# One store moved from ScalarE's DMA queue to SyncE's, behind the last load, in a split-GELU kernel

## The chip, the cores and the metric

The kernel runs on one core of a Trainium2 chip. The metric is the time on the device in microseconds (us), the median of several runs.

The core has five instruction engines. Three matter here: ScalarE (ACT in the profile) computes GELU, VectorE (DVE) multiplies, SyncE (SP) only issues DMAs. A DMA issued by SyncE stands in the profile's queue q1, one issued by ScalarE in q10. All queues are served by the core's 16 DMA engines. A DMA engine moves its part of a DMA in packets, and ends it with a packet of 4 bytes, called its closing write here: the 35 DMAs of the kernel before leave 560 of them, 16 each. In the traces a DMA lands with its last closing write (the store of tile 14 in the kernel before: closing write at 459.3 us, landing at 459.4).

## The reference

```python
x: (32, 512, 2048) float32
x1, x2 = x[..., :1024], x[..., 1024:]
out = 0.5 * x1 * (1 + erf(x1 / sqrt(2))) * x2     # (32, 512, 1024) float32
```

The input is 134 MB and the output 67 MB. There are only two elementwise steps between them.

## The kernel before

The input is cut into 16 tiles. A tile has 128 partitions with 8 rows of 2048 numbers each: 8 MB in, 4 MB out. Two buffers hold input tiles and two hold output tiles. SyncE issues the loads, two tiles ahead. ScalarE issues the stores, except those of the last tile, which go to SyncE in four pieces of 1 MB as the pieces become ready.

```python
xpool = ctx.enter_context(tc.tile_pool(name="xpool", bufs=2))
opool = ctx.enter_context(tc.tile_pool(name="opool", bufs=2))

def load(i):
    x_tile = xpool.tile([P, R, dim], x.dtype, name="x_tile")
    nc.sync.dma_start(out=x_tile, in_=x_t[i])
    return x_tile

ahead = [load(0), load(1)]
for i in range(n_tiles):                       # 16 tiles, R = 8
    x_tile = ahead.pop(0)
    o_tile = opool.tile([P, R, half], out.dtype, name="o_tile")
    last = i == n_tiles - 1
    pieces = 4 if last else 1
    step = R // pieces
    for k in range(pieces):
        for r in range(k * step, (k + 1) * step):
            nc.scalar.activation(              # GELU in place
                out=x_tile[:, r, :half], in_=x_tile[:, r, :half], func=GELU
            )
            nc.vector.tensor_mul(
                out=o_tile[:, r, :],
                in0=x_tile[:, r, :half], in1=x_tile[:, r, half:],
            )
        rows = slice(k * step, (k + 1) * step)
        queue = nc.sync if last else nc.scalar
        queue.dma_start(out=o_t[i][:, rows, :], in_=o_tile[:, rows, :])
    if i + 2 < n_tiles:
        ahead.append(load(i + 2))
```

Of the kernel before, what the change touches and what calls it, by code (L numbers as in the profile page):

```python
# [1 line left out]

# [4 lines left out]

GELU = mybir.ActivationFunctionType.Gelu


@with_exitstack
def kernel(
    ctx: ExitStack,
    tc: tile.TileContext,
    x: bass.AP,
    out: bass.AP,
):




    nc = tc.nc
    P = nc.NUM_PARTITIONS

    x_flat = x.flatten_outer_dims()
    out_flat = out.flatten_outer_dims()
    n_rows, dim = x_flat.shape
    half = dim // 2

    R = 8  # L30
    x_t = x_flat.rearrange("(n p r) d -> n p r d", p=P, r=R)
    o_t = out_flat.rearrange("(n p r) d -> n p r d", p=P, r=R)
    n_tiles = x_t.shape[0]
# [10 lines that stand above are left out]
    for i in range(n_tiles):  # L44
# [7 lines that stand above are left out]
                nc.scalar.activation(  # L52
# [4 lines that stand above are left out]
                    in0=x_tile[:, r, :half],  # L57
                    in1=x_tile[:, r, half:],
                )
            rows = slice(k * step, (k + 1) * step)  # L60
            queue = nc.sync if last else nc.scalar
            queue.dma_start(out=o_t[i][:, rows, :], in_=o_tile[:, rows, :])
        if i + 2 < n_tiles:
            ahead.append(load(i + 2))


# [1 line left out]
_INS = ['x']  # L68
_OUTS = [((32, 512, 1024), 'float32')]


# [23 lines left out]
```

## Time and profile before

The time was 472.1 us (472.06 to 473.35 in 3 runs). This is what matters, and where it is read:

| what | value | view |
|---|---|---|
| span of the profiled run | 470.3 us | page |
| VectorE / ScalarE busy | 31% / 26% | page, part 1 |
| bytes moved | 201.35 MB, mean 428 GB/s | page, part 2 |
| rate in a tile period of 29.0 us | 434 GB/s | windows |
| packet time of the two data queues, per DMA engine | 467.2 us | packet records |
| issue of load 15 to its landing | 47.65 us | chain of waits |
| closing wait of SyncE for the last store | 5.4 us | waits of SyncE |

From the page of the kernel before: the DMA row gives the mean busy share of the 16 DMA engines in tenths (9 is 90% or more) for 40 equal slices of the span. A queue line gives packets, megabytes and share of the 16 engines' time.

```profile
DVE  0070704307042070520606116060250702407034
DMA  8999999999999999999999999999999999999998
...
q1 hardware_dynamic: 2880, 138.41, 68.4%
q10 hardware_dynamic: 2160, 62.92, 31.0%
HBM read 134.22 MB, written 67.11 MB: 428 GB/s over the span
...
out_dram<-o_tile SPq DMA_DIRECT2D x4, 1024.0 KB, 5.6
```

(Names like L62 are lines of the kernel; edits make the numbers a few higher in other runs.) The two queues together take 99.4% of the DMA engines' time, and VectorE rests most of the time. The windows view of the kernel before shows a middle stretch; after the busy times of the engines come the DMA share and the rate in GB/s:

```profile
347.50:376.50 29.00, 9.17 (x8) 7.68 (x8) 0.00 (x0) 1.00 1.00 434
376.50:405.50 29.00, 9.17 (x8) 7.68 (x8) 0.00 (x0) 1.00 1.00 434
```

The DMA engines are full (1.00). The Trainium skill, "DMA: Bandwidth & Descriptors", section "Specifications", gives 435 GB/s as the ceiling of the fabric, and the measured 434 GB/s is next to it.

The chain of waits gives the last load as start, length, and what:

```profile
405.50 47.65 DMA x_tile<-in_x_dram
```

The timeline of the kernel before shows the end (start, length, engine, instruction, and in brackets how long the engine had been idle and what ended it):

```profile
434.50 0.34 ACTq L62 DMA_DIRECT2D out_dram<-o_tile  x1
453.23 7.68 ACT L52 ACTIVATE x_tile<-x_tile 128x1024 f32<-128x1024 f32 x8 [21.34 <-DMA x_tile<-in_x_dram]
454.32 9.17 DVE L55 TENSOR_TENSOR o_tile<-x_tile 128x1024 f32<-128x1024 f32 x8 [19.85 <-ACT x_tile L52]
456.70 7.14 SPq L62 DMA_DIRECT2D out_dram<-o_tile  x4
```

The first line is the store of tile 14 on ScalarE's queue. Tile 15 is computed from 453.23 to 463.5 us. The last small store is issued at 463.5 us (the fourth of the last line, which ends at 463.84). After it SyncE waits for the last landing, in its view of waits (total, times, longest):

```profile
SPq L90 <- DMA out_dram<-o_tile: 5.4, 1, 5.4
```

### The profile page before, as it was taken

The page shows a single profiled execution, that of the slowest core. Times are in us where ns is not written, and L with a number is a line of the kernel's source. Part 1 is how long each engine was busy: PE and PEld are TensorE (multiplying, and loading weights), DVE is VectorE, ACT ScalarE, POOL GpSimd, SP SyncE. Part 2 cuts the span into 40 slices and gives each one's busy share as a digit, 9 for nine tenths or more (in the row PEclk, how much of TensorE's full clock was granted, in tenths as well). Part 3 has the DMA queues.
Part 4 walks back from the last instruction along what each step waited for, and adds up shares of the span by engine and source line. Part 5 has one row for each costly group of instructions (what it writes and reads, how often), then busy time and mean ns, then how long its engine had stood idle before and what let it go on. Part 6 is the DMA issues. An engine that isn't in the chain of part 4 may idle for free.

```text
span 470.3 us, 408 instructions
## 1 busy us (share of the span) xinstructions
DVE 146.7 (31%) x128; ACT 124.2 (26%) x129; POOL 0.2 (0%) x4
## 2 busy tenths in 40 slices
DVE  0070704307042070520606116060250702407034
ACT  1050605106050150601406024060330603206042
POOL 0000000000000000000000000000000000000000
DMA  8999999999999999999999999999999999999998
GB/s 357 446 446 382 429 443 424 463 404 443 426 446 421 443 415 449 413 443 424 457 429 435 438 438 415 426 438 435 440 440 418 449 438 435 424 443 432 418 410 351
DMA packets 5042, 201.35 MB, mean 428 GB/s; under 512 B 560, under 2 KB 560, under 8 KB 560
## 3 DMA queue, kind: packets, MB, share of 16 engines
q1 hardware_dynamic: 2880, 138.41, 68.4%
q10 hardware_dynamic: 2160, 62.92, 31.0%
q14 instruction: 2, 0.02, 0.0%
HBM read 134.22 MB, written 67.11 MB: 428 GB/s over the span
## 4 chain that ended last, share of the span: by engine, by line
DMA 81%; DVE 15%; ACT 2%; DVEq 0%; issue 0%; SPq 0%; ACTq 0%
DMA x_tile<-in_x_dram 81%; DVE o_tile L55 15%; ACT x_tile L52 2%; DVEq L90 0%; SPq L40 0%; ACTq L52 0%
## 5 line engine op out<-in xcount | busy, mean ns | idle before, releaser
L55 DVE TENSOR_TENSOR o_tile<-x_tile 128x1024 f32<-128x1024 f32 x128 | 146.7, 1218 | 316.8 <-ACT x_tile L52 316.8
L52 ACT ACTIVATE x_tile<-x_tile 128x1024 f32<-128x1024 f32 x128 | 122.9, 1042 | 336.0 <-DMA x_tile<-in_x_dram 336.0
L52 ACT ACT_TABLE_LOAD x1 | 1.3, 1283 | 0.7 <-PEq L79 0.7
L79 POOL MEMSET const-bfloat16-1.0<- 128x1 bf16 x1 | 0.1, 102 | 0.0
L79 POOL MEMSET const-uint8-127<- 128x1 uint8 x1 | 0.1, 102 | 0.0
L79 POOL MEMSET const-float32-1.0<- 128x1 f32 x1 | 0.1, 99 | 0.0
L79 POOL MEMSET const-float32-0.0<- 128x1 f32 x1 | 0.1, 98 | 0.2 <-issue 0.2
## 6 DMA issues: line engine op xcount, KB each, us to landing
out_dram<-o_tile ACTq DMA_DIRECT2D x15, 4096.0 KB, 39.4
out_dram<-o_tile SPq DMA_DIRECT2D x4, 1024.0 KB, 5.6
x_tile<-in_x_dram SPq DMA_DIRECT2D x16, 47.6
```

Of the source, the lines that this page charges most:

```text
L52: nc.scalar.activation(out=x_tile[:, r, :half], in_=x_tile[:, r, :half], func=GELU)
L55: nc.vector.tensor_mul(out=o_tile[:, r, :], in0=x_tile[:, r, :half], in1=x_tile[:, r, half:],)
L79: nc = _bacc.Bacc("TRN2", target_bir_lowering=False, num_devices=1)
```

## The change

The idea is to get the store of tile 14 out of the way of the last load. On ScalarE's queue it alternates with that load, packet by packet. Behind the load in SyncE's own queue it has to wait until the load is through. The last tile should then arrive and be computed earlier.

```diff
             rows = slice(k * step, (k + 1) * step)
-            queue = nc.sync if last else nc.scalar
+            queue = nc.sync if i >= n_tiles - 2 else nc.scalar
             queue.dma_start(out=o_t[i][:, rows, :], in_=o_tile[:, rows, :])
```

## The prediction

> **What bounds the kernel now.** The 16 DMA engines. The page gives 201.35 MB at a mean of 428 GB/s over the 470.3 us span; the DMA row shows 9 in 38 of 40 slices. Summed over the packet records of the two data queues, packet time is 467.2 us per engine. The first packet starts at 2.1 us and the last ends at 469.4 us, so no engine is ever without work. VectorE is busy 31%, ScalarE 26%. The chain of waits names x_tile loads for 81%, but a load lasts 47.6 us only because it shares the engines with stores; the windows view shows 434 GB/s in each 29.0 us tile period.
>
> **How the two queues share.** The Trainium skill, "DMA: Bandwidth & Descriptors", sections "Issuing engines are not separate DMA queues" and "Queues, rings and completion order", says that all issuing engines' DMAs run on the same 16 DMA engines, each taking its queues in turn, packet by packet. This trace agrees: while both queues have work, an engine alternates a 65,536-byte load packet (2.418 us) with a 32,768-byte store packet (1.213 us).
>
> **What the change moves.** Nothing is removed or added: the 4 MB store of tile 14 goes from ScalarE's queue to SyncE's, behind load 15 and ahead of tile 15's four 1 MB stores. Its issue stays at 434.5 us, when VectorE ends tile 14: SyncE issued load 15 at 405.5 us and is free.
>
> On the DMA engines only the order changes. Store 13 empties ScalarE's queue at 441.9 to 444.8 us. Now store 14 alternates with load 15 from there; after the change load 15 has the engines to itself. On the slowest engines three store packets (3 x 1.213 = 3.6 us) leave its path. Load 15 should land at about 449.7 us, not 453.14 (44.2 us after issue, not 47.65). Tile 15's GELU and multiply move 3.4 us earlier, and VectorE ends near 460.1 us, not 463.5.
>
> **How much is critical.** None. Already now the last 1 MB store is issued at 463.5 us and waits behind others of its queue until 466.9 us, so 3.4 us of lead only lengthens that wait. After load 15, store 14 needs 8 x 1.213 = 9.7 us per engine and ends at about 459.4 us, as now; the four small stores need 4 x 2.45 us and end at 469.4 us, as now. One gap exists: eight engines end store 14 early and take about 1.2 us for their first 8 KB packet, not 0.309. It may vanish, but the engines that end last don't have it, so at most some tenths come off.
>
> **Predicted time.** 472.0 us, 8 times in 10 within 471.2 to 473.0. Chances: faster by over 2% 0.01, within 2% 0.97, slower by over 2% 0.02.
>
> **What the profile would show.** Right: load 15 lands 44 to 45 us after issue; the idle time of ScalarE before tile 15 falls from 21.3 to about 18 us; ScalarE's queue is empty from about 445 us; the four small stores take 7 to 9 us to land instead of 5.6; the store of tile 14 lands 25 us after issue, as now; total packet time and the last landing stay. Wrong: a gap in the DMA engines between load 15 and store 14, or an issue on SyncE held up.
>
> **What would make it wrong.** If switching from load to store within one queue leaves the engines idle (about 1 us); if one queue alone moves large packets slower than two together; if SyncE's queue cannot hold load 15, store 14 and the small stores, and a late issue opens a gap at the end.

## The result, and the profile after

After the change the median was 471.81 us (471.47 to 472.24, 4 runs), before 472.22 us over 4 runs, one of them run beside the kernel after. The ratio is 0.9987, 95% interval 0.9969 to 1.0005: no difference is shown. Ratios here and below are the mean time of one kernel's runs over that of the other's runs of the same rounds, so not quite the ratio of the medians quoted. Executions over 1.5% slower than the fastest of the same kernel are left out of the means.

The lines of the page that answer to those of before:

```profile
DVE  0070704307052070520705216061150702507061
DMA  8999999999999999999999999999999999999987
...
q1 hardware_dynamic: 3024, 142.61, 70.4%
q10 hardware_dynamic: 2016, 58.72, 28.9%
HBM read 134.22 MB, written 67.11 MB: 428 GB/s over the span
...
out_dram<-o_tile SPq DMA_DIRECT2D x1, 4096.0 KB, 24.7
out_dram<-o_tile SPq DMA_DIRECT2D x4, 1024.0 KB, 8.9
```

4.2 MB have moved from q10 to q1, and the sum is the same. The small stores now land 8.9 us after their issue instead of 5.6. The last load in the chain of waits, and the end in the timeline:

```profile
406.07 43.98 DMA x_tile<-in_x_dram
```

```profile
435.06 25.70 SPq L63 DMA_DIRECT2D out_dram<-o_tile  x5
450.14 7.68 ACT L53 ACTIVATE x_tile<-x_tile 128x1024 f32<-128x1024 f32 x8 [17.68 <-DMA x_tile<-in_x_dram]
451.23 9.17 DVE L56 TENSOR_TENSOR o_tile<-x_tile 128x1024 f32<-128x1024 f32 x8 [16.19 <-ACT x_tile L53]
```

The load came 3.67 us sooner (47.65 - 43.98), and VectorE ended at 460.4 us instead of 463.5. (The whole trace after is shifted by 0.57 us at the issue of load 15, 406.07 against 405.50, which is why the two differences are not the same.) The closing wait of SyncE, in its view of waits:

```profile
SPq L91 <- DMA out_dram<-o_tile: 8.7, 1, 8.7
```

So the last store is issued 3.1 us earlier (463.84 against 435.06 + 25.70 = 460.76 us, where its issue ends), and SyncE waits 3.3 us longer for it (8.7 - 5.4); the last landing is 0.2 us later in this trace.

The packet records (start, duration, size and queue of each DMA packet, put on the same time axis by the landing of load 15) say why:

| packet records | before | after |
|---|---|---|
| packet time of the two data queues, per engine | 467.2 us | 467.1 us |
| first packet starts / last packet ends | 2.1 / 469.4 us | 2.1 / 469.5 us |
| last closing write of the load 15 | 453.1 us | 450.1 us |
| last closing write of the store of tile 14 | 459.3 us | 459.7 us |
| longest 8 KB packet | 1.387 us | 0.309 us |

The DMA engines had the same packets to do and did them one after the other, in another order. The load moved forward and the store's packets back.

One small thing did change. Before, on eight engines the first 8 KB packet of tile 15's first store took 0.985 to 1.387 us instead of 0.309; after, none did. The five engines that ended last before (469.16 to 469.36 us) all had such a packet; the last engine without one ended at 469.14 us. So by this trace some tenths of a microsecond could come off. After, 15 engines had ended by 468.9 us, and one ended at 469.5 us. The times (0.6 us less, interval 1.5 less to 0.2 more) do not show whether anything came off.

### The profile page after: what moved, and what is told of

It reads as the page before. It is cut to its first block, busy times and chain, and to the rows that moved or that the text cites. A ratio compares the mean times of both kernels' runs of the same rounds, so it can differ in the third digit from the quotient of the medians.

```text
span 470.5 us, 408 instructions
## 1 busy us (share of the span) xinstructions
DVE 146.7 (31%) x128; ACT 124.2 (26%) x129; POOL 0.2 (0%) x4
## 4 chain that ended last, share of the span: by engine, by line
DMA 80%; DVE 15%; ACT 2%; DVEq 0%; issue 0%; SPq 0%; ACTq 0%
DMA x_tile<-in_x_dram 80%; DVE o_tile L56 15%; ACT x_tile L53 2%; DVEq L91 0%; SPq L41 0%; ACTq L53 0%
## 6 DMA issues: line engine op xcount, KB each, us to landing
out_dram<-o_tile SPq DMA_DIRECT2D x1, 4096.0 KB, 24.7
```

## The experiments

Two explanations stand against each other. The theory: while the DMA engines are full, the order of their packets is free, and the lead of the last tile's compute is kept as slack, time by which the last store could be issued later without harm. The rivals: the lead was worth something and was eaten, either by a single queue being slower than two or by the small stores standing behind the large one; or the last tile's compute has nothing to do with the end at all. Except where the text says otherwise each was timed in 5 rounds against the kernel before (before_mul6 and after_half14 have 4 runs).

| run | median us | ratio to before (95%) |
|---|---|---|
| before_mul3 | 474.12 | 1.0036 (1.0023 to 1.0048) |
| after_mul3 | 472.31 | 0.9998 (0.9985 to 1.0010) |
| before_mul6 | 477.83 | 1.0114 (1.0100 to 1.0128) |
| after_mul6 | 474.36 | 1.0043 (1.0030 to 1.0057) |
| before_half14 | 469.27 | 0.9937 (0.9925 to 0.9950) |
| after_half14 | 467.42 | 0.9895 (0.9881 to 0.9908) |
| pieces_pool | 472.56 | 1.0005 (0.9992 to 1.0019) |
| pieces_scalar | 472.22 | 0.9991 (0.9978 to 1.0005) |
| all_sync | 475.40 | 1.0067 (1.0054 to 1.0080) |
| sync_last4 | 472.96 | 1.0014 (1.0000 to 1.0028) |
| sync_last8 | 474.13 | 1.0033 (1.0021 to 1.0046) |
| all_sync_again | 475.84 | one look only, state unknown |

### Where the lead went: slack, measured by delaying the compute

The multiply of the last row of tile 15 is done 4 or 7 times instead of once, which delays the last store and changes no result. It was done to both kernels. The edit, shortened:

```diff
-                nc.vector.tensor_mul(...)
+                for _ in range(4 if last and r == R - 1 else 1):   # mul6: 7
+                    nc.vector.tensor_mul(...)
```

> Before, with the multiply of the last row of tile 15 done 4 times instead of once (right result): VectorE ends 3 x 1.22 = 3.66 us later, at 467.2 us. Theory: the last small store has about 0.8 us of slack before the change (it could start at 466.9 us, and an issue needs about 2.6 us to its first data), so it lands 5.3 us after its issue, at 472.5 us, and the time grows by about 3 us to 475.1 us. Rival (the compute of the last tile is no part of the end at all): no change.

> After, with the same 3 multiplies more: VectorE ends at 464.1 us. Theory: the slack is now about 4 us, so nothing is lost: 472.0 us, at most 0.3 us more. The 3.4 us that the change won are here, as slack. Rival (the gain was lost to something else, a slower queue, and isn't kept as slack): as much slower as before_mul3.

> Before, with the multiply of the last row of tile 15 done 7 times: VectorE ends 7.3 us later, at 470.8 us. Theory: the last store lands at 476.1 us, time about 478.8 us.

> After, with the same 6 multiplies more: VectorE ends at 467.7 us. Theory: the last store lands at 473.0 us, time about 475.6 us: 3.2 us less than before_mul6, the whole of what the change won for the last tile's compute.

All four were correct. The same delay cost the kernel before 1.7 us and 5.4 us, the kernel after nothing and 2.0 us (each the ratio less one, times the mean of before, 472.4 us). The direction of each was as expected; the growth expected over 472.1 us was 1.3 to 1.5 us too large in three of four. The reason is one term. An issue into an empty queue was expected to land 5.3 us later, the shortest value in the kernel before. That value still contained waiting. With the queue really empty it is 3.8 us: the timeline and the closing wait of before_mul6 show it,

```profile
454.32 16.73 DVE L56 TENSOR_TENSOR o_tile<-x_tile 128x1024 f32<-128x1024 f32 x14 [19.81 <-ACT x_tile L52]
456.70 14.70 SPq L63 DMA_DIRECT2D out_dram<-o_tile  x4
```

```profile
SPq L91 <- DMA out_dram<-o_tile: 3.4, 1, 3.4
```

and so does the listing of that line's DMAs, with the shortest, median and longest time to landing:

```profile
DMA to landing us min/median/max: 3.8/5.5/24.6
```

With the queue empty the closing wait was 3.4 us, in before_mul3, before_mul6 and after_mul6 alike. What it is longer is slack: 5.4 - 3.4 = 2.0 us before, 8.7 - 3.4 = 5.3 us after. The waits of after_mul3 and after_mul6 agree, 5.0 us with part of the slack used and 3.4 us with all of it:

```profile
SPq L92 <- DMA out_dram<-o_tile: 5.0, 1, 5.0
SPq L92 <- DMA out_dram<-o_tile: 3.4, 1, 3.4
```

The multiplies held VectorE 12.95 - 9.17 = 3.78 us (timeline of before_mul3) and 16.73 - 9.17 = 7.56 us longer:

```profile
454.39 12.95 DVE L56 TENSOR_TENSOR o_tile<-x_tile 128x1024 f32<-128x1024 f32 x11 [19.84 <-ACT x_tile L52]
```

The slack taken from these gives what should be lost:

| | delay | less slack | measured |
|---|---|---|---|
| before_mul3 | 3.78 | 1.8 | 1.7 |
| before_mul6 | 7.56 | 5.6 | 5.4 |
| after_mul3 | 3.78 | 0 | -0.1 |
| after_mul6 | 7.56 | 2.3 | 2.0 |

The rival that the last tile's compute has no part in the end falls with before_mul6, and the one that the lead was lost to something else falls with after_mul3. The change did what it was made to do, and 3.3 us of slack is what it bought.

### When the lead is worth time

Only rows 0 to 3 of tile 14 are stored, in both kernels. Their outputs are wrong, which doesn't matter for the times. It takes 2 MB of store out of the place where the lead was hidden.

```diff
             rows = slice(k * step, (k + 1) * step)
+            if i == n_tiles - 2:
+                rows = slice(0, R // 2)
```

> Before, but only rows 0 to 3 of 8 of tile 14 are stored (wrong result on purpose): 2 MB, 4 x 1.213 = 4.85 us of packet time per engine, are taken away. Theory: load 15 still alternates with the store and lands at about 453 us, VectorE ends at 463.5 us, and the last small store then finds an empty queue and lands 5.3 us later, at 468.8 us: only 0.6 us come off, 471.5 us. Rival (time follows the bytes whatever the order): 467.3 us.

> After the change, with the same 2 MB of tile 14 not stored (wrong result on purpose). Theory: load 15 lands at 450 us, VectorE ends at 460.4 us, the last small store lands about 5.3 us later, at 465.7 us: about 3.7 us come off, 468.2 us. So with the DMA engines no longer full at the end, the change is worth about 3.3 us (before_half14 against this). Rival (the earlier compute is of no worth at all, whatever else): the same time as before_half14.

The time went down by 3.0 us in the kernel before and by 5.0 us in the kernel after, so with the DMA engines no longer full at the end the change is worth 2.0 us (medians: 469.27 against 467.42, 1.85 us). That is the direction expected, but both sizes were misjudged: 0.6, 3.7 and 3.3 us were expected. The windows view of before_half14, the stretch after load 15 landed:

```profile
452.00:456.00 4.00, 2.80 (x3) 3.89 (x5) 0.00 (x0) 1.00 0.21 90
456.00:460.00 4.00, 4.00 (x4) 3.79 (x5) 0.00 (x0) 1.00 0.93 387
```

and the same of after_half14:

```profile
452.00:456.00 4.00, 4.00 (x5) 4.00 (x5) 0.00 (x0) 1.00 0.80 336
456.00:460.00 4.00, 4.00 (x4) 1.54 (x2) 0.00 (x0) 1.00 1.03 426
```

Before, the DMA engines stand at 0.21 of their time for 4 us, because there is nothing left to do until tile 15's first piece is ready. After, the store of tile 14 fills that place. The kernel after took off 5.0 us for 4.8 us of packet time per engine (8 packets of 1.213 us became 8 of 0.611 us). It was not quite full to the end, though: 15 of its engines paused between 453.3 and 454.7 us, for 0.2 to 1.3 us, until the first small store's packets came. From there the packets of the four small stores follow one another to the end, 454.6 to 464.7 us, and in before_half14 likewise from 456.8 to 467.0 us. So in both it is the first of the four small stores, not the last, whose start sets the end; it was issued at 455.59 us before and 453.33 us after, 2.3 us earlier. The kernel before took off more than expected for two reasons. The half store goes in 8 packets of 16 KB per engine, not in 4 of 32 KB, so it takes a smaller part of each turn from load 15, which now lands after 45.82 us instead of 47.65 us, in the chain of waits:

```profile
406.21 45.82 DMA x_tile<-in_x_dram
```

(3 store packets x 0.602 us shorter = 1.8 us.) And the landing after the last issue was again taken as 5.3 us; here SyncE's closing wait is 4.1 us (3.4 us with an empty queue), since the last store still stands behind the others.

### Would the small stores have to overtake the large one?

The four stores of tile 15 were given another queue than the store of tile 14. First GpSimd's:

```diff
-            queue = nc.sync if i >= n_tiles - 2 else nc.scalar
+            queue = nc.gpsimd if last else nc.sync if i == n_tiles - 2 else nc.scalar
```

> As after the change, but the four 1 MB stores of tile 15 go to GpSimd's queue, so that they need not wait behind the store of tile 14 but alternate with it. Theory: the small stores land earlier than the 8.9 us of after, but the store of tile 14 ends later by as much; 472 us within 0.3%, up to 1 us more if GpSimd's queue starts late. Rival (the 3.4 us won for tile 15's compute are lost only because its stores stand in one queue behind the store of tile 14): 469 us.

It gave 472.56 us, the same as before. But it isn't the test it was meant to be: the packet records show the first small store starting only 4.9 us after its issue, when the store of tile 14 was down to its last packets. So a second run used ScalarE's queue, which was empty by then (the edit shortened):

```diff
+            if last:   # on ScalarE's queue, piece k - 1 is issued after piece k's GELUs
+                if k > 0:
+                    nc.scalar.dma_start(<rows of piece k - 1>)
+                if k == pieces - 1:
+                    nc.scalar.dma_start(<rows of piece k>)
+                continue
             queue = nc.sync if i >= n_tiles - 2 else nc.scalar
```

> pieces_pool did not do what it was meant to: GpSimd's queue took 4.9 us to its first packet, when the store of tile 14 was nearly done. Here the small stores go to ScalarE's empty queue, each issued one piece late so that ScalarE does not stop for VectorE: the first should start near 455 us, in the middle of the store of tile 14, and alternate with it. Theory (order is free while the DMA engines are full): the first small store lands 1 us or more earlier than in after (462.1 us), the store of tile 14 ends about 1.2 us later (4 small packets of 0.309 us in between), the last small store lands at 469.4 us as ever, and the time is 472.2 us within 0.3%. Rival (the lead of tile 15's compute is lost only because its stores stand behind that of tile 14 in one queue): about 469 us.

The time was 472.22 us, as expected, but again the small stores hardly overtook. The timeline of pieces_scalar has the first of them issued at

```profile
453.87 0.34 ACTq L65 DMA_DIRECT2D out_dram<-o_tile  x1
```

and its first packet starts at 458.2 us, 4.3 us later, not near 455 us. It got between the last packets of the store of tile 14, which ended 1.0 us later than after the change (460.7 against 459.7 us), and landed no earlier for it (462.5 against 462.2 us). In before_mul6, where the engines were idle, the first packet came 1.2 us after the issue (472.3 after 471.1). The first store of the kernel before is like pieces_scalar: issued by ScalarE at 32.93 us, while a load keeps the engines busy, it has its first packet at 37.6 us, 4.7 us later. So in these traces a queue that had just been filled did not get its turn at once while another one kept the engines busy; 4 to 5 us of the other's packets went first. (The 1.2 us are of SyncE's queue; no run measured ScalarE's or GpSimd's with idle engines.) The Trainium skill, "DMA: Bandwidth & Descriptors", section "Queues, rings and completion order", has the engine take its queues in turn packet by packet. In the middle of this kernel the records agree (one 64 KB packet, one 32 KB packet, and so on); at the start of a queue they show this delay beside it.

What follows: giving the small stores their own queue brings nothing, in two runs. Whether they would bring something if they really overtook remains open. The sum of packet times says no, but no run here shows it.

### Is one queue as good as two? The miss

> Every store, not only that of tile 14, goes to SyncE's queue, so loads and stores follow one another in one queue all through: 16 changes from load to store where the change made one. Theory (the DMA engines are never without work, so the order of the same packets is free): 472.0 us, within 0.3% of before, load 15 landing near 450 us as after the change. Rival (one queue that carries both loads and stores loses time at each change of direction, and this ate the gain of the change): about 1 us or more per tile, so 485 us or more.

```diff
-            queue = nc.sync if i >= n_tiles - 2 else nc.scalar
+            queue = nc.sync
```

This expectation failed. Moving every store to SyncE's queue took 475.40 us, 3.2 us more than before by the ratio. It isn't the 13 us of the rival, but the order is not entirely free. The page of all_sync shows the DMA row full except for its last slice:

```profile
DMA  8999999999999999999989999999999999999996
```

The mean over the 16 engines hides where the loss is. The closing writes of each DMA, one per engine, show it: some engines fall behind the others. Three more runs measured how it grows:

> The stores of the last 4 tiles go to SyncE's queue (3 whole-tile stores where the change moved one), the others stay on ScalarE's. all_sync moved 15 and took 3.0 us more, with one DMA engine ending 0.9 us after all others and 3.9 us after the first. If each turn from load to store in one queue costs the same, 3 of 15 give 0.6 us more than before: 473.0 us. If the cost comes only after many turns (in all_sync the spread of the engines began to grow at about the sixth load): 472.4 us, as before.

> The stores of the last 8 tiles go to SyncE's queue: 7 whole-tile stores. If each turn costs the same: 1.4 us more than before, 473.8 us. If the cost comes only after about six turns: at most 0.5 us more.

> all_sync once more, for a second trace: if the late DMA engine is what this order makes and no accident of one execution, the spread of the 16 engines' closing writes grows again from about 0.5 us at the first loads to over 3 us at load 15, and the time is 475 to 476 us; before keeps its spread near 2 us from the second load on.

Their edits are `n_tiles - 4` and `n_tiles - 8` in place of `n_tiles - 2`, and all_sync unchanged.

| kernel | large stores on SyncE's queue | time over before | mean end of the 16 engines after the first packet | slowest engine's end after the median engine's |
|---|---|---|---|---|
| before | 0 | 0 | 466.9 us | 0.35 us |
| after | 1 | -0.6 (interval -1.5 to 0.2) | 466.4 us | 1.1 us |
| sync_last4 | 3 | 0.7 us | 466.6 us | 2.0 us |
| sync_last8 | 7 | 1.6 us | 467.1 us | 3.0 us |
| all_sync | 15 | 3.2 us | 467.1 us | 3.4 us |
| all_sync_again | 15 | one look | 467.5 us | 4.2 us |

(The times are the ratio less one, times the mean of before in those rounds.) Divided by the number of stores it is 0.22, 0.22 and 0.21 us each. That fits a cost in proportion. The interval of sync_last4 (0 to 1.3 us) would also allow no cost at all; that of sync_last8 (1.0 to 2.2 us) excludes the "at most 0.5 us" of the alternative, a cost only after six turns. The mean end of the engines moves by about 1 us at most, and the slowest one falls back. In all_sync the spread of the closing writes over the 16 engines grows from 0.5 us at load 0 to 3.9 us at load 15, in all_sync_again from 0.9 to 4.5 us, while before keeps about 2.15 us at its loads from the second on. The slow packets are mostly the last 64 KB load packets before the queue turns to a store, up to 3.15 us instead of 2.418 us in all_sync and up to 3.50 us in sync_last8. Why those packets are slow is open, and so is whether the one queue or the order that comes with it makes them slow: the runs changed both.

For the change itself this would mean 0.2 us for its one store, an estimate from these runs. That lies inside its interval and can't be seen: the trace after has no slow packet at that turn. About half of its 1.1 us in the last column is one 2.95 us packet at 197 us, long before the changed store; a packet like it stands in the trace of before at 199 us.

## Why the prediction was right

A forecast of no change can come true for many reasons, so its steps count for more than its time. The time predicted was 472.0 us, within 471.2 to 473.0; measured were 471.81 us. Point by point:

- "The 16 DMA engines" bound the kernel. Right: after_half14 took off 5.0 us for 4.8 us of packet time, and the delays of compute cost nothing until the slack was used.
- "Load 15 should land [...] 44.2 us after issue, not 47.65." Right: 43.98 us. Counting the store packets that stand between the load's packets on the slowest DMA engine gave the size.
- VectorE "ends near 460.1 us". Right: 460.4 us in a trace that was 0.6 us late.
- "How much is critical. None." Right within the noise: SyncE's closing wait grew from 5.4 to 8.7 us when the issue moved by 3.1 us, and after_mul3 shows the lead kept as slack.
- The idle time of ScalarE before tile 15 falls "to about 18 us": 17.68. Small stores land after "7 to 9 us": 8.9. The store of tile 14 lands "25 us after issue": 24.7. Total packet time stays: 467.2 and 467.1 us.
- The late first 8 KB packets on eight engines "may vanish" and bring at most some tenths. They vanished (longest 8 KB packet 0.309 us instead of 1.387). The reason given, "the engines that end last don't have it", was wrong: the five that ended last all had it. That no more than some tenths hung on it was luck, since an engine without it ended only 0.2 us before the last one.
- Of the three things that would make it wrong, the second ("if one queue alone moves large packets slower than two together") proved real, at 0.2 us for each large store. For one store it is too small to matter. The other two did not show: no gap at the turn to the store in the trace after, and no late issue.

What else I had wrong was in the experiments: the 5.3 us from an issue into an empty queue to landing (3.8 measured), the packets of a half store (half as large, not half as many), and that order within one queue is wholly free.

No run suggested a version faster than both kernels. What would be left is the packet time itself: the first packet starts 2.1 us after the span's start, the last ends 0.9 us before its end, and between them the engines are full, but not always fast: in the trace before, slow load packets between 30 and 45 us, up to 3.6 us instead of 2.418, cost an engine 1.2 us on average. No run tried to remove them.

## What to carry to other kernels

A chain of waits that names loads for 80% of the span does not say that an earlier load helps; ask first whether the DMA engines have a gap that the earlier load would close. Here they had next to none, and the new order of the same bytes only moved slack about. The closing wait for the last store, less the time that a store takes in an empty queue, measures that slack directly: here 2.0 us before and 5.3 us after. The same change is worth having where the end of the kernel is not filled by stores (2.0 us with half a store less), but don't carry the pattern through the whole kernel without measuring: all stores behind the loads in one queue cost 3.2 us.

## What the Trainium skill lacked or had wrong

- "DMA: Bandwidth & Descriptors", section "Issuing engines are not separate DMA queues", says that issuing from several engines only saves the time of the sequencer. Here it saved more: 15 stores of 4 MB put into the loads' queue cost 3.2 us by the ratio (medians 475.40 against 472.41 us), 0.21 us each, while SyncE spent 447.5 of 473.1 us waiting for VectorE, so its issue time was not what ran short; the slowest DMA engine ended 3.4 us after the median one. Putting them there also changed the order of the packets; what of the two costs is open.
- "DMA: Bandwidth & Descriptors", section "Queues, rings and completion order", says nothing of when a newly filled queue gets its first turn while another one is busy. With the engines busy on another queue the first packet came 4.3 and 4.7 us (ScalarE's queue) and 4.9 us (GpSimd's) after the issue; with idle engines 1.2 us (SyncE's).
- No page looked up here gives the time from the issue of a 1 MB store by SyncE to its landing ("DMA: Bandwidth & Descriptors" fits a time to the size only for DMAs issued by GpSimd): 3.8 us in an empty queue, of which its packets take 2.5 us.
